# A row-mean kernel: two neighbouring rows per partition, three buffers, and a last block in shrinking chunks

## The chip, the cores and the metric

The kernel runs on one core of one Trainium2 chip. The metric is device time in microseconds (us), the median of several runs. All runs quoted here were classed as fast ones at a full granted clock. A time that is called "in the span" counts from the first instruction of the profiled run; the span is some 1.7 us shorter than the measured time.

Loads and stores go through 16 DMA engines. One load instruction becomes a number of packets on each engine: in the bulk loads of these runs 8, 16 or 64. For each load, and for the final store, the trace also records 16 completion counts; the transfer counts as landed when the last of them has come. DVE is the vector engine, ACT the scalar engine, PE the matrix engine, and SP issues the DMAs.

## The reference

```python
# x: float32, 64 x 256 x 8192 (537 MB, standard normal)
def reference(x):
    return np.mean(x, axis=2)          # 64 x 256
```

There are 16384 rows of 8192 numbers (32 KiB a row). Each number is read once and added up.

## The kernel before

A bulk load brings 128 partitions x 2 rows, 8 MiB. The two rows of a partition lie 128 rows apart in memory. DVE sums the first one, ACT the second one. There are two buffers. The last two row tiles (a tile is one row on each of 128 partitions) are handled apart, and the very last one comes in four chunks through two small buffers.

```python
x_v = x.rearrange("b c s -> (b c) s").rearrange("(t p) s -> p t s", p=P)
# ... cut ...
in_pool   = ctx.enter_context(tc.tile_pool(name="in", bufs=2))
part_pool = ctx.enter_context(tc.tile_pool(name="part", bufs=2))
# ... cut ...
while t < nbulk:                                   # nbulk = T - 2 = 126
    n = min(R, nbulk - t)                          # R = 2
    xt = in_pool.tile([P, n, S], x.dtype)
    nc.sync.dma_start(out=xt[:], in_=x_v[:, t : t + n, :])          # L82
    for j in range(n):
        tt = t + j
        if (tt % 2) == 0:
            dve_reduce(res_d[:, tt : tt + 1], xt[:, j, :])          # tensor_reduce, L61
        else:
            act_reduce(res_a[:, tt : tt + 1], xt[:, j, :])          # activation with accum_out, L70
    t += n
# ... cut ...
xt = in_pool.tile([P, S], x.dtype)
nc.sync.dma_start(out=xt[:], in_=x_v[:, t1, :])                     # L94; halves to DVE and ACT
# ... cut ...
for c in range(4):
    xc = part_pool.tile([P, q], x.dtype)                            # q = 2048
    nc.sync.dma_start(out=xc[:], in_=x_v[:, t2, c * q : (c + 1) * q])   # L108
    fn, dst = targets[c]                                            # DVE, ACT, DVE, ACT
    fn(dst, xc[:])
# add the partial sums of the last tile on DVE and on ACT, transpose res_d and res_a
# on PE into one PSUM tile (adding them), scale on DVE, store 128 rows of 512 bytes (L134)
```

## Time and profile before

| | before |
|---|---|
| median time | 1259.3 us (1259.16 to 1259.45) |
| span of the profiled run | 1257.8 us |
| load queue busy, share of 16 engines | 99.3% |
| DVE busy, ACT busy | 44%, 36% |
| one bulk load lands every | 19.43 us |
| last chunk in use from, to the end of the span | 1252.03 us, 5.78 us |

First the page of the profiled run: the DMA share in 40 slices (9 is 90% or more), the bytes moved in the same slices, the count of packets, and the load queue with packets, MB and share of 16 engines' span.

```profile
DMA  9999999999999999999999999999999999999996
GB/s 402 431 433 434 433 434 434 432 431 426 430 430 434 432 434 433 434 432 431 427 430 430 434 433 432 433 434 432 431 427 431 430 434 431 434 434 433 432 431 259
DMA packets 18004, 536.97 MB, mean 427 GB/s; under 512 B 1104, under 2 KB 1232, under 8 KB 1232
...
q1 hardware_dynamic: 18000, 536.94, 99.3%
```

The loads are the limit from the second slice to the last but one. Only the first and the last slice show a hole.

Next the timeline of DVE in the middle of the run: start, duration, instruction, and in brackets how long it was idle and what ended that.

```profile
605.91 8.69 DVE L61 TENSOR_REDUCE res_d<-xt 128x1 f32<-128x8192 f32 x1 [10.74 <-DMA xt<-in_x_dram]
625.33 8.69 DVE L61 TENSOR_REDUCE res_d<-xt 128x1 f32<-128x8192 f32 x1 [10.74 <-DMA xt<-in_x_dram]
```

DVE waits for each load, and the loads come 19.42 us apart, 8 MiB each: 432 GB/s. In the packet records all bulk packets have 32768 bytes and last 1218 ns (median). DVE frees a buffer 8.7 us after it landed. At that moment the other load has 10.7 us to go, so the refill is queued in time.

The end looks otherwise. This is the chain of waits from 1238 us on (start, duration, what), followed by the busy times of 1240 to 1245 us (the last two columns are the DMA share and GB/s).

```profile
1244.58 0.33 SPq L108
...
1245.01 6.94 DMA xc<-in_x_dram
...
1252.03 2.01 ACT junk L70 x2
...
1254.07 0.30 ACT res_a L115
...
1254.41 0.49 PE resT_ps L128
...
1254.92 0.29 DVE resT L133
```

```profile
1240.00:1245.00 5.00, 0.00 (x0) 0.00 (x0) 4.56 (x2) 3.72 (x4) 0.00 (x0) 1.00 0.21 88
```

The third and fourth chunks of the last tile are issued at 1244.58 and 1245.01 us only, after DVE and ACT have freed the two small buffers. By then the queue has run dry: 88 GB/s in these 5 us. After the last chunk come ACT, ACT, PE, DVE in a row, then the store. The list of DMA issues gives the store's size and its time from issue to landing, 1.5 us:

```profile
out_dram<-resT SPq DMA_DIRECT2D x1, 64.0 KB, 1.5
```

By the timeline of SP it is issued at 1255.24 us:

```profile
1255.24 0.35 SPq L134 DMA_DIRECT2D out_dram<-resT  x1
```

### The profile page before, as it was taken

Reading aid. Unit: us, or ns where it says so; the run is one execution under the profiler, and the core shown is the slowest. Engines: PE = TensorE matmul, PEld = TensorE weight load, DVE = VectorE, ACT = ScalarE, POOL = GpSimd, SP = SyncE. Lnnn points to the kernel's source line nnn. Section 1 sums busy time; section 2 is a strip of 40 time slices with the busy share of each in tenths; the row PEclk is TensorE's granted clock in tenths of the full one; section 3 lists DMA queues with packets and bytes.
Section 4 is the critical chain, followed back from the end, with each engine's and each line's share of the span. In section 5 each row is a group of like instructions: output and inputs, shape, how many; then the busy total and the mean of one; then the engine's idle time right before and its main releaser. Section 6 shows DMA issues by size and latency. Waiting matters only on the chain.

```text
span 1257.8 us, 460 instructions
## 1 busy us (share of the span) xinstructions
PE 0.9 (0%) x2; PEld 0.4 (0%) x2; DVE 556.6 (44%) x68; ACT 458.0 (36%) x134; POOL 1.0 (0%) x8
## 2 busy tenths in 40 slices
PE   0000000000000000000000000000000000000000
PEld 0000000000000000000000000000000000000000
DVE  2354353453543534435345354353443544535435
ACT  2244243342432423424334243243342433424424
POOL 0000000000000000000000000000000000000000
DMA  9999999999999999999999999999999999999996
GB/s 402 431 433 434 433 434 434 432 431 426 430 430 434 432 434 433 434 432 431 427 430 430 434 433 432 433 434 432 431 427 431 430 434 431 434 434 433 432 431 259
DMA packets 18004, 536.97 MB, mean 427 GB/s; under 512 B 1104, under 2 KB 1232, under 8 KB 1232
## 3 DMA queue, kind: packets, MB, share of 16 engines
q1 hardware_dynamic: 18000, 536.94, 99.3%
q14 instruction: 4, 0.03, 0.0%
HBM read 536.87 MB, written 0.07 MB: 427 GB/s over the span
## 4 chain that ended last, share of the span: by engine, by line
DMA 77%; DVE 22%; issue 0%; ACT 0%; SPq 0%; PE 0%; ACTq 0%
DMA xt<-in_x_dram 77%; DVE res_d L61 22%; DMA xc<-in_x_dram 1%; ACT junk L70 0%; SPq L82 0%; PE resT_ps L128 0%; SPq L108 0%; ACT res_a L115 0%; DVE resT L133 0%; SPq L94 0%; ACTq L70 0%
## 5 line engine op out<-in xcount | busy, mean ns | idle before, releaser
L61 DVE TENSOR_REDUCE res_d<-xt 128x1 f32<-128x8192 f32 x64 | 551.6, 8619 | 690.7 <-DMA xt<-in_x_dram 690.7
L70 ACT ACTIVATE junk<-xt 128x8192 f32<-128x8192 f32 x64 | 446.5, 6976 | 765.3 <-DMA xt<-in_x_dram 765.3
L70 ACT ACTIVATION_READ_ACCUMULATOR junk<-xt 128x1 f32 x64 | 11.9, 186 | 0.0
L70 ACT ACT_TABLE_LOAD x1 | 1.3, 1283 | 22.7 <-DMA xt<-in_x_dram 22.7
L70 ACT ACTIVATE junk<-xc 128x2048 f32<-128x2048 f32 x2 | 3.8, 1910 | 8.3 <-DMA xc<-in_x_dram 8.3
L61 DVE TENSOR_REDUCE aux_d<-xc 128x1 f32<-128x2048 f32 x1 | 2.3, 2286 | 4.9 <-DMA xc<-in_x_dram 4.9
L61 DVE TENSOR_REDUCE res_d<-xc 128x1 f32<-128x2048 f32 x1 | 2.3, 2276 | 0.0
L133 DVE TENSOR_SCALAR resT<-resT_ps 128x128 f32<-128x128 f32 x1 | 0.3, 292 | 3.0 <-PE resT_ps L128 3.0
L124 PE MATMUL resT_ps<-ident,res_d 128*128 128x128 f32 x1 | 0.4, 447 | 1252.1 <-DVE res_d L112 1252.1
L124 PEld LDWEIGHTS resT_ps<-ident,res_d 128*128 128x128 f32 x1 | 0.2, 182 | 1252.1 <-issue 1252.1
L128 PE MATMUL resT_ps<-ident,res_a 128*128 128x128 f32 x1 | 0.5, 472 | 1.8 <-ACT res_a L115 1.8
L70 ACT ACTIVATION_READ_ACCUMULATOR junk<-xc 128x1 f32 x2 | 0.4, 187 | 0.0
L115 ACT ACTIVATE res_a<-res_a,aux_a 128x1 f32<-128x1 f32 x1 | 0.3, 295 | 0.0
L48 POOL TENSOR_SCALAR_AFFINE_SELECT ident<-ident 128x128 f32<-128x128 f32 x1 | 0.3, 292 | 0.1
L40 POOL MEMSET res_d<- 128x128 f32 x1 | 0.2, 204 | 0.3 <-POOLq L149 0.3
L41 POOL MEMSET res_a<- 128x128 f32 x1 | 0.2, 204 | 0.0
L47 POOL MEMSET ident<- 128x128 f32 x1 | 0.2, 204 | 0.0
L128 PEld LDWEIGHTS resT_ps<-ident,res_a 128*128 128x128 f32 x1 | 0.2, 183 | 2.1 <-ACT res_a L115 2.1
L112 DVE TENSOR_TENSOR res_d<-res_d,aux_d 128x1 f32<-128x1 f32 x1 | 0.2, 159 | 0.0
L149 POOL MEMSET const-bfloat16-1.0<- 128x1 bf16 x1 | 0.1, 101 | 0.0
L149 POOL MEMSET const-uint8-127<- 128x1 uint8 x1 | 0.1, 101 | 0.0
L149 POOL MEMSET const-float32-0.0<- 128x1 f32 x1 | 0.1, 98 | 0.2 <-issue 0.2
(1 smaller groups left out, 0.1 us busy)
## 6 DMA issues: line engine op xcount, KB each, us to landing
xt<-in_x_dram SPq DMA_DIRECT2D x63, 8192.0 KB, 30.1
xt<-in_x_dram SPq DMA_DIRECT2D x1, 4096.0 KB, 20.9
xc<-in_x_dram SPq DMA_DIRECT2D x4, 1024.0 KB, 15.0
out_dram<-resT SPq DMA_DIRECT2D x1, 64.0 KB, 1.5
```

The source lines that it names most:

```text
L40: nc.gpsimd.memset(res_d[:], 0.0)
L41: nc.gpsimd.memset(res_a[:], 0.0)
L47: nc.gpsimd.memset(ident[:], 0.0)
L48: nc.gpsimd.affine_select(out=ident[:], in_=ident[:], compare_op=mybir.AluOpType.not_equal, fill=1.0, base=0, pattern=[[-1, P]], channel_m ...
L61: nc.vector.tensor_reduce(out=dst, in_=src, axis=mybir.AxisListType.X, op=mybir.AluOpType.add,)
L70: nc.scalar.activation(out=junk[:], in_=src, func=mybir.ActivationFunctionType.Copy, accum_out=dst,)
L112: nc.vector.tensor_add(out=res_d[:, t2 : t2 + 1], in0=res_d[:, t2 : t2 + 1], in1=aux_d[:, 0:1])
L115: nc.scalar.activation(out=res_a[:, t2 : t2 + 1], in_=res_a[:, t2 : t2 + 1], func=mybir.ActivationFunctionType.Identity, bias=aux_a[:, 0:1 ...
L124: nc.tensor.matmul(out=resT_ps[:], lhsT=res_d[:], rhs=ident[:], is_transpose=True, start=True, stop=False,)
L128: nc.tensor.matmul(out=resT_ps[:], lhsT=res_a[:], rhs=ident[:], is_transpose=True, start=False, stop=True,)
L133: nc.vector.tensor_scalar_mul(out=resT[:], in0=resT_ps[:], scalar1=inv)
L149: nc = _bacc.Bacc("TRN2", target_bir_lowering=False, num_devices=1)
```

## The change

The intent: longer contiguous pieces for the loads (64 KiB per partition in place of 2 x 32 KiB), one more buffer so that loads are queued further ahead (ACT writes over its source, which frees the scratch tile's space), and a last block whose loads are all queued at once and shrink toward the end, so that little is left to do after the last byte.

```diff
-    x_v = x.rearrange("b c s -> (b c) s").rearrange("(t p) s -> p t s", p=P)
+    x_v = x.rearrange("b c s -> (b c) s").rearrange("(n p r) s -> n p r s", p=P, r=R)
-    in_pool = ctx.enter_context(tc.tile_pool(name="in", bufs=2))
+    in_pool = ctx.enter_context(tc.tile_pool(name="in", bufs=BULK_BUFS))     # 3
 # ... cut ...
+    def act_sum(dst, src):
+        nc.scalar.activation(out=src, in_=src, func=COPY, accum_out=dst)
+    for n in range(LB):                                                      # LB = 63
+        xt = in_pool.tile([P, R, S], x.dtype, name="xt")
+        nc.sync.dma_start(out=xt[:], in_=x_v[n])
+        dve_sum(res[0][:, n : n + 1], xt[:, 0, :])
+        act_sum(res[1][:, n : n + 1], xt[:, 1, :])
 # ... cut: the last block, one bulk buffer xl: its first row in one load, halves to DVE and ACT
+    for c, w in enumerate(LAST_CHUNKS[:-1]):                # (4096, 2048, 1024, 512, 512)
+        ld = nc.sync.dma_start(out=xl[:, 1, pos : pos + w], in_=x_v[LB, :, 1, pos : pos + w])
+        mid = pos + w // 2                                  # half to DVE, half to ACT
+        dve_sum(fin_in[:, lastw + k : lastw + k + 1], xl[:, 1, pos:mid])
+        act_sum(fin_in[:, lastw + k + 1 : lastw + k + 2], xl[:, 1, mid : pos + w])
 # ... cut: the loop's counters k and pos
+    with tc.issue_after(ld.ins):
+        nc.sync.dma_start(out=fin_in[:, 0:lastw], in_=x_v[LB, :, 1, pos:S])
 # ... cut: the 63 bulk blocks' sums are transposed on PE, scaled on DVE and stored (out_bulk)
+    nc.vector.tensor_scalar(out=fin_in[:, 0 : lastw + k], in0=fin_in[:, 0 : lastw + k],
+        scalar1=inv, scalar2=None, op0=mybir.AluOpType.mult, op1=ADD, accum_out=fin[:, 1:2])
+    nc.sync.dma_start(out=out_last, in_=fin[:])             # 128 pieces of 8 bytes, side by side
```

More of the change, by code (lines that the diff above doesn't have):

```diff
@@ L6 @@
 from concourse._compat import with_exitstack
-TILES_PER_DMA = 2
+ROWS = 2
+BULK_BUFS = 3
+LAST_CHUNKS = (4096, 2048, 1024, 512, 512)
 @with_exitstack
@@ L19 @@
     P = nc.NUM_PARTITIONS
+    F32 = mybir.dt.float32
+    X = mybir.AxisListType.X
+    ADD = mybir.AluOpType.add
+    COPY = mybir.ActivationFunctionType.Copy
     B, C, S = x.shape
     N = B * C
-    assert N % P == 0, (N, P)
-    T = N // P
-    x_v = x.rearrange("b c s -> (b c) s").rearrange("(t p) s -> p t s", p=P)
-    outT_v = out.rearrange("b c -> (b c)").rearrange("(t p) -> t p", p=P)
-    R = TILES_PER_DMA
-    assert T >= 2
-    in_pool = ctx.enter_context(tc.tile_pool(name="in", bufs=2))
-    part_pool = ctx.enter_context(tc.tile_pool(name="part", bufs=2))
-    res_pool = ctx.enter_context(tc.tile_pool(name="res", bufs=1))
-    junk_pool = ctx.enter_context(tc.tile_pool(name="junk", bufs=1))
-    psum_pool = ctx.enter_context(tc.tile_pool(name="psum", bufs=1, space=bass.MemoryType.PSUM))
-    res_d = res_pool.tile([P, T], mybir.dt.float32)
-    res_a = res_pool.tile([P, T], mybir.dt.float32)
-    nc.gpsimd.memset(res_d[:], 0.0)
-    nc.gpsimd.memset(res_a[:], 0.0)
-    aux_d = res_pool.tile([P, 4], mybir.dt.float32)
-    aux_a = res_pool.tile([P, 4], mybir.dt.float32)
-    ident = res_pool.tile([P, P], mybir.dt.float32)
+    R = ROWS
+    assert R == 2 and N % (P * R) == 0, (N, P, R)
+    NB = N // (P * R)
+    LB = NB - 1
+    assert 1 <= LB <= P and sum(LAST_CHUNKS) == S
+    inv = 1.0 / float(S)
+    x_v = x.rearrange("b c s -> (b c) s").rearrange("(n p r) s -> n p r s", p=P, r=R)
+    o_v = out.rearrange("b c -> (b c)")
+    out_bulk = o_v[0 : LB * P * R].rearrange("(n p r) -> n p r", p=P, r=R)
+    out_last = o_v[LB * P * R : N].rearrange("(p r) -> p r", r=R)
+    in_pool = ctx.enter_context(tc.tile_pool(name="in", bufs=BULK_BUFS))
+    res_pool = ctx.enter_context(tc.tile_pool(name="res", bufs=1))
+    psum_pool = ctx.enter_context(
+        tc.tile_pool(name="psum", bufs=1, space=bass.MemoryType.PSUM)
+    )
+    res = [res_pool.tile([P, NB], F32, name=f"res{r}") for r in range(R)]
+    ident = res_pool.tile([P, P], F32)
     nc.gpsimd.memset(ident[:], 0.0)
@@ L56 @@
     )
-    inv = 1.0 / float(S)
-    def dve_reduce(dst, src):
-        nc.vector.tensor_reduce(
-            out=dst,
-            in_=src,
-            axis=mybir.AxisListType.X,
-            op=mybir.AluOpType.add,
-        )
-    def act_reduce(dst, src):
-        junk = junk_pool.tile([P, src.shape[-1]], mybir.dt.float32)
-        nc.scalar.activation(
-            out=junk[:],
-            in_=src,
-            func=mybir.ActivationFunctionType.Copy,
-            accum_out=dst,
-        )
@@ L77 @@
-    nbulk = T - 2
-    t = 0
-    while t < nbulk:
-        n = min(R, nbulk - t)
-        xt = in_pool.tile([P, n, S], x.dtype)
-        nc.sync.dma_start(out=xt[:], in_=x_v[:, t : t + n, :])
-        for j in range(n):
-            tt = t + j
-            if (tt % 2) == 0:
-                dve_reduce(res_d[:, tt : tt + 1], xt[:, j, :])
-            else:
-                act_reduce(res_a[:, tt : tt + 1], xt[:, j, :])
-        t += n
-    t1 = T - 2
-    half = S // 2
-    xt = in_pool.tile([P, S], x.dtype)
@@ L94 @@
-    nc.sync.dma_start(out=xt[:], in_=x_v[:, t1, :])
-    dve_reduce(res_d[:, t1 : t1 + 1], xt[:, 0:half])
-    act_reduce(res_a[:, t1 : t1 + 1], xt[:, half:S])
-    t2 = T - 1
-    q = S // 4
-    targets = [
-        (dve_reduce, res_d[:, t2 : t2 + 1]),
-        (act_reduce, res_a[:, t2 : t2 + 1]),
-        (dve_reduce, aux_d[:, 0:1]),
-        (act_reduce, aux_a[:, 0:1]),
-    ]
-    for c in range(4):
-        xc = part_pool.tile([P, q], x.dtype)
-        nc.sync.dma_start(out=xc[:], in_=x_v[:, t2, c * q : (c + 1) * q])
-        fn, dst = targets[c]
-        fn(dst, xc[:])
@@ L112 @@
-    nc.vector.tensor_add(
-        out=res_d[:, t2 : t2 + 1], in0=res_d[:, t2 : t2 + 1], in1=aux_d[:, 0:1]
-    )
-    nc.scalar.activation(
-        out=res_a[:, t2 : t2 + 1],
-        in_=res_a[:, t2 : t2 + 1],
-        func=mybir.ActivationFunctionType.Identity,
-        bias=aux_a[:, 0:1],
-        scale=1.0,
-    )
-    resT_ps = psum_pool.tile([T, P], mybir.dt.float32)
-    nc.tensor.matmul(
-        out=resT_ps[:], lhsT=res_d[:], rhs=ident[:], is_transpose=True,
-        start=True, stop=False,
-    )
@@ L128, with dve_sum @@
-    nc.tensor.matmul(
-        out=resT_ps[:], lhsT=res_a[:], rhs=ident[:], is_transpose=True,
-        start=False, stop=True,
-    )
-    resT = res_pool.tile([T, P], mybir.dt.float32)
-    nc.vector.tensor_scalar_mul(out=resT[:], in0=resT_ps[:], scalar1=inv)
-    nc.sync.dma_start(out=outT_v, in_=resT[:])
+    def dve_sum(dst, src):
+        nc.vector.tensor_reduce(out=dst, in_=src, axis=X, op=ADD)
+    def act_sum(dst, src):
+        nc.scalar.activation(out=src, in_=src, func=COPY, accum_out=dst)
@@ new lines @@
+    for n in range(LB):
[3 more added lines that the diff above has]
+        act_sum(res[1][:, n : n + 1], xt[:, 1, :])
+    nparts = 2 * len(LAST_CHUNKS)
+    lastw = LAST_CHUNKS[-1]
+    xl = in_pool.tile([P, R, S], x.dtype, name="xt")
+    fin_in = res_pool.tile([P, lastw + nparts], F32)
+    fin = res_pool.tile([P, R], F32)
+    head = res_pool.tile([P, 2], F32)
+    half = S // 2
@@ new lines @@
+    nc.sync.dma_start(out=xl[:, 0, :], in_=x_v[LB, :, 0, :])
+    dve_sum(head[:, 0:1], xl[:, 0, 0:half])
+    act_sum(head[:, 1:2], xl[:, 0, half:S])
+    pos, k = 0, 0
+    for c, w in enumerate(LAST_CHUNKS[:-1]):
+        ld = nc.sync.dma_start(
+            out=xl[:, 1, pos : pos + w], in_=x_v[LB, :, 1, pos : pos + w]
+        )
+        mid = pos + w // 2
+        dve_sum(fin_in[:, lastw + k : lastw + k + 1], xl[:, 1, pos:mid])
+        act_sum(fin_in[:, lastw + k + 1 : lastw + k + 2], xl[:, 1, mid : pos + w])
+        k += 2
+        pos += w
@@ new lines @@
+    with tc.issue_after(ld.ins):
+        nc.sync.dma_start(out=fin_in[:, 0:lastw], in_=x_v[LB, :, 1, pos:S])
+    nc.vector.tensor_scalar(
+        out=head[:],
+        in0=head[:],
+        scalar1=inv,
+        scalar2=None,
+        op0=mybir.AluOpType.mult,
+        op1=ADD,
+        accum_out=fin[:, 0:1],
+    )
+    bulk = res_pool.tile([P, P, R], F32)
+    for r in range(R):
+        ps = psum_pool.tile([P, P], F32, name=f"ps{r}")
+        nc.tensor.transpose(out=ps[:LB, :], in_=res[r][:, 0:LB], identity=ident[:])
+        nc.vector.tensor_scalar_mul(out=bulk[:LB, :, r], in0=ps[:LB, :], scalar1=inv)
@@ L138 @@
+    nc.sync.dma_start(out=out_bulk, in_=bulk[:LB])
+    nc.vector.tensor_scalar(
+        out=fin_in[:, 0 : lastw + k],
+        in0=fin_in[:, 0 : lastw + k],
+        scalar1=inv,
+        scalar2=None,
+        op0=mybir.AluOpType.mult,
+        op1=ADD,
+        accum_out=fin[:, 1:2],
+    )
+    nc.sync.dma_start(out=out_last, in_=fin[:])
 _INS = ['x']
```

## The prediction

> **What bounds the kernel now.** The DMA engines. The page's queue table has the load queue busy for 99.3% of 16 engines' span, 427 GB/s on average; DVE is busy for 44%, ACT for 36%. The 40 slices show 426 to 434 GB/s, but 402 in the first and 259 in the last. In the chain of waits an 8 MiB load lands every 19.43 us (431.8 GB/s). A buffer is refilled 8.7 us (the DVE reduction) after it lands, while 10.7 us of the other load are still queued, so the queue never runs dry in the bulk. In the packet records every bulk packet is 32768 bytes and takes 1218 ns (median).
>
> **What the change does.**
>
> 1. *Descriptors.* Two neighbouring rows make one contiguous 64 KiB run per partition: 8 packets per engine and load in place of 16. Packets of 8192 bytes take 309 ns (median), of 32768 1218: a line through both gives 6 ns per packet. Eight packets saved, times 63 loads, times 6 ns: 3.0 us. [...] Estimate: 3.2 us, all on the critical path.
>
> 2. *Third buffer, sums in place.* They remove nothing critical: 0. ACT's 7.03 us stays off the path.
>
> 3. *End of the loading.* Before, the last row's chunks share two buffers: the third load waits for a DVE reduction, the fourth is issued at 1245.01 us after ACT, and the windows show 88 GB/s in 1240 to 1245 us. With a full queue the last chunk would land 9.75 us (4 MiB) after 1237.9, at 1247.7, not 1252.03. The change queues all the last block's loads ahead: -4.3 us; smaller chunks cost +0.2.
>
> 4. *After the last byte.* Before, 1252.03 to 1257.8 us: ACT 2.01 (two instructions), ACT 0.30, PE 0.49, DVE 0.29, then some 2.6 of output issue, landing and exit. After: one DVE instruction over 520 elements, estimated 0.7 us from 2.29 for 2048, then the same 2.6. Transposes and bulk output finish while the last block loads. -2.4 us, less 0.1 for 8-byte output pieces.
>
> 5. *Start.* Unchanged: the first load is in at 22.7 us.
>
> **Sum.** 1259.3 - 3.2 - 4.3 + 0.2 - 2.3 = 1249.7 us, 0.8% less. Range for 8 in 10: 1246.5 to 1252.5. Faster by over 2%: 1%; within 2%: 97%; slower by over 2%: 2%.
>
> **What the profile would show.** Load packets of 65536 bytes, about 2430 ns each; a load landing every 19.38 us; no low slice before the end, and no DMA issue of the last block waiting for DVE or ACT of the same block; the last load landing about 1244.8 us into the span; 3.4 us from there to the end.
>
> **What would make it wrong.** The run is cut back into 32 KiB packets, or longer packets cost proportionally as much (about 1253). Reading partitions 64 KiB apart is slower or faster in HBM: 1% of rate is 12 us. One engine lags and the last small chunk waits for it. The bulk output delays the final one. ACT's small sums, each with a 0.19 us accumulator read, end later than DVE's.

## The result, and the profile after

The changed kernel takes 1249.59 us (median of 4 runs, 1249.44 to 1249.93), against 1259.30 us before (4 runs). A ratio here is the mean time of one kernel's fast runs over the mean of the other's of the same rounds, so it is not quite the ratio of the two medians. It is 0.9923, with a 95% interval of 0.9909 to 0.9937. The predicted 1249.7 us is met within 0.1 us. The question is whether it was met for the right reasons.

The same lines of the page, for the changed kernel:

```profile
DMA  9999999999999999999999999999999999999997
GB/s 403 437 437 437 437 437 437 422 420 435 437 437 437 437 437 435 437 426 418 435 437 437 437 437 437 433 437 428 418 435 437 437 437 437 435 433 437 431 418 336
DMA packets 10156, 536.97 MB, mean 430 GB/s; under 512 B 1257, under 2 KB 1320, under 8 KB 1704
...
q1 hardware_dynamic: 10152, 536.94, 99.5%
```

There are some 7800 fewer packets. Don't read the single slices too finely: they jump between 418 and 437 GB/s while the loads go on landing evenly. The timeline of DVE is the better measure:

```profile
603.77 8.69 DVE L61 TENSOR_REDUCE res<-xt 128x1 f32<-128x8192 f32 x1 [10.66 <-DMA xt<-in_x_dram]
623.13 8.69 DVE L61 TENSOR_REDUCE res<-xt 128x1 f32<-128x8192 f32 x1 [10.67 <-DMA xt<-in_x_dram]
```

A load now lands every 19.35 us (19.36 between these two). The packets have 65536 bytes and last 2422 ns (median).

The end, from the timeline of SP and from the chain of waits, then the same 5 us of busy times:

```profile
1193.42 0.33 SPq L80 DMA_DIRECT2D xt<-in_x_dram  x1
1193.80 1.85 SPq L86 DMA_DIRECT2D xt<-in_x_dram  x4
1195.69 0.43 SPq L95 DMA_DIRECT2D fin_in<-in_x_dram  x1
```

```profile
1195.69 47.63 DMA fin_in<-in_x_dram
...
1243.46 0.69 DVE fin_in L114
```

```profile
1240.00:1245.00 5.00, 0.00 (x0) 0.00 (x0) 3.71 (x6) 2.74 (x8) 0.00 (x0) 1.00 0.41 152
```

All six loads of the last block are issued by 1196 us, some 47 us before the last of them lands at 1243.32. The 152 GB/s are no hole in the loading any more: the loading itself ends within these 5 us. One DVE instruction follows, at 1243.46. Then the store, first from the timeline, then from the list of DMA issues:

```profile
1244.19 0.37 SPq L123 DMA_DIRECT2D out_dram<-fin  x1
```

```profile
out_dram<-fin SPq DMA_DIRECT2D x1, 1.0 KB, 3.1
```

This store is 64 times smaller than the one before, and takes 3.1 us to land where the other took 1.5.

The three stretches of the two spans, cut at the same events (the start of the first reduction, of the last full block's, and of the instruction that uses the last chunk):

| stretch | before, us | after, us | change | predicted |
|---|---|---|---|---|
| to the first reduction | 22.71 | 22.68 | 0.0 | 0 |
| 62 more bulk loads | 1205.0 | 1200.7 | -4.3 | -3.2 |
| last block, to the use of its last chunk | 24.3 | 20.1 | -4.2 | -4.1 |
| from there to the end | 5.8 | 4.7 | -1.1 | -2.3 |
| sum | 1257.8 | 1248.2 | -9.7 | -9.6 |

Two terms of the sum were off by more than 1 us each, in opposite directions. (These are single executions, and the profiled one of the changed kernel was the slowest of its four, 1249.93 us against 1249.44 for the fastest, so a few tenths of a us in a stretch mean little.) The experiments ask what sets each term.

### The profile page after: what moved, and what is told of

Its sections match the earlier page's. It is cut to its first block, busy times and chain, and to the rows that moved or that the text cites. A ratio compares the mean times of both kernels' runs of the same rounds, so it can differ in the third digit from the quotient of the medians.

```text
span 1248.2 us, 464 instructions
## 1 busy us (share of the span) xinstructions
PE 0.9 (0%) x2; PEld 0.4 (0%) x2; DVE 557.5 (45%) x74; ACT 458.0 (37%) x137; POOL 0.7 (0%) x6
## 4 chain that ended last, share of the span: by engine, by line
DMA 85%; DVE 15%; SPq 0%; issue 0%; DVEq 0%
DMA xt<-in_x_dram 81%; DVE res L61 15%; DMA fin_in<-in_x_dram 4%; SPq L86 0%; DVE fin_in L114 0%; SPq L68 0%; SPq L80 0%; DVEq L114 0%; DVEq L149 0%
## 5 line engine op out<-in xcount | busy, mean ns | idle before, releaser
L61 DVE TENSOR_REDUCE res<-xt 128x1 f32<-128x8192 f32 x63 | 547.2, 8686 | 684.8 <-DMA xt<-in_x_dram 684.8
L64 ACT ACTIVATE xt<-xt 128x8192 f32<-128x8192 f32 (+2 forms) x68 | 450.5, 6625 | 784.4 <-DMA xt<-in_x_dram 784.3
L64 ACT ACTIVATION_READ_ACCUMULATOR xt<-xt 128x1 f32 x68 | 12.7, 187 | 0.0
L61 DVE TENSOR_REDUCE fin_in<-xt 128x1 f32<-128x2048 f32 (+3 forms) x4 | 4.6, 1154 | 0.8 <-DMA xt<-in_x_dram 0.6
L61 DVE TENSOR_REDUCE head<-xt 128x1 f32<-128x4096 f32 x1 | 4.4, 4420 | 0.2 <-DMA xt<-in_x_dram 0.2
```

Source lines behind the costliest of these rows:

```text
L61: nc.vector.tensor_reduce(out=dst, in_=src, axis=X, op=ADD)
L64: nc.scalar.activation(out=src, in_=src, func=COPY, accum_out=dst)
```

## The experiments

Every kernel was timed beside the kernel before on the same chip (medians of 1259.15 to 1259.39 us there). The starting theory: a fixed cost per packet explains the bulk, queueing ahead explains the last block, and the third buffer does nothing.

### Rows apart again (e1_rows_apart)

```diff
-    ... .rearrange("(n p r) s -> n p r s", p=P, r=R)
+    ... .rearrange("(n r p) s -> n p r s", p=P, r=R)
```

> The changed kernel, but the two rows that a partition takes in a bulk load lie 128 rows apart in memory, as before the change: packets of 32768 bytes again, everything else (three buffers, sums in place, the new end) kept. The output is in the wrong order on purpose. Theory A (a fixed cost of about 9 ns per packet): a load lands every 19.43 us instead of 19.35, 1249.6 + 62 x 0.07 = 1254.0 us. Rival B (the gain of the bulk came from the third buffer, not from the packets): stays at 1249.6.

Measured: 1254.33 us (1254.10 to 1254.94). All bulk packets have 32768 bytes again. The timeline of DVE:

```profile
605.61 8.69 DVE L61 TENSOR_REDUCE res<-xt 128x1 f32<-128x8192 f32 x1 [10.74 <-DMA xt<-in_x_dram]
625.03 8.69 DVE L61 TENSOR_REDUCE res<-xt 128x1 f32<-128x8192 f32 x1 [10.74 <-DMA xt<-in_x_dram]
```

The loads are 19.42 us apart again, with three buffers. The bulk gain came from the rows, not from the buffer. But "two rows that are neighbours" means two things at once: longer packets, and longer contiguous reading in memory.

### Neighbouring rows, but a cut in the destination (e2_cut_dest)

```diff
-        xt = in_pool.tile([P, R, S], x.dtype, name="xt")
-        nc.sync.dma_start(out=xt[:], in_=x_v[n])
+        xt = in_pool.tile([P, R, S + 16], x.dtype, name="xt")
+        nc.sync.dma_start(out=xt[:, :, 0:S], in_=x_v[n])
 # ... cut: the sums and the last block leave out the gap in the same way
```

> The changed kernel with the same neighbouring rows read, 64 KiB in a piece from memory, but each partition's buffer has a gap of 64 bytes between the two rows, so that no packet can be longer than 32768 bytes. Theory A (cost per packet): 1254.0 us, a load every 19.43 us, as in the run with rows apart. Rival C (longer contiguous reading in memory is what is faster, whatever the packets): 1249.6 us, 19.35 us per load.

Measured: 1253.77 us (1253.70 to 1254.27), correct output. The packets have 32768 bytes though 64 KiB in a piece are read. Of every three loads in the middle of the run, two land 19.43 or 19.44 us after the one before and one 19.37; the median of all 62 periods is 19.42:

```profile
605.96 8.69 DVE L61 TENSOR_REDUCE res<-xt 128x1 f32<-128x8192 f32 x1 [10.74 <-DMA xt<-in_x_dram]
625.40 8.69 DVE L61 TENSOR_REDUCE res<-xt 128x1 f32<-128x8192 f32 x1 [10.75 <-DMA xt<-in_x_dram]
644.77 8.69 DVE L61 TENSOR_REDUCE res<-xt 128x1 f32<-128x8192 f32 x1 [10.69 <-DMA xt<-in_x_dram]
```

It is the packets that count, not the neighbourhood in memory. The reading order is that of the changed kernel, and the gain is gone. (The gap also moves the second row within the buffer. The run before this one, and the one with packets of 8 KiB below, have no gap and show the cost too.)

### Two buffers (e3_two_bufs)

```diff
-BULK_BUFS = 3
+BULK_BUFS = 2
```

> The changed kernel with two bulk buffers in place of three. Theory: the queue holds 10.7 us of work at each refill, so nothing changes, 1249.6 us, within 0.4, and the end of the loading too. Rival B (the third buffer carries part of the gain): above 1251 us, with gaps in the DMA or a later landing of the last block.

Measured: 1249.77 us (1249.57 to 1250.19), correct. The last block's loads are now issued later, between 1212.85 and 1215.55 us, but that is still 28 us before the last chunk lands. The timeline of SP:

```profile
1212.85 0.33 SPq L80 DMA_DIRECT2D xt<-in_x_dram  x1
1213.23 1.85 SPq L86 DMA_DIRECT2D xt<-in_x_dram  x4
1215.12 0.43 SPq L95 DMA_DIRECT2D fin_in<-in_x_dram  x1
```

The third buffer carries none of the gain.

### The rows alone, in the kernel before (e4_before_pairs)

```diff
+    x_pair = x.rearrange("b c s -> (b c) s").rearrange("(n p r) s -> n p r s", p=P, r=2)
-        nc.sync.dma_start(out=xt[:], in_=x_v[:, t : t + n, :])
+        nc.sync.dma_start(out=xt[:], in_=x_pair[t // 2])
```

> The kernel before with one part of the change alone: each bulk load takes two neighbouring rows per partition (64 KiB packets); two buffers, scratch tile and the old end stay. Output in the wrong order on purpose. Theory A: 62 x 0.07 = 4.3 us off, 1255.0 us. Rival B (third buffer): 1259.3, unchanged.

Measured: 1254.81 us (1254.40 to 1255.18), 4.5 us less than the kernel before. The period of the changed kernel is there, with two buffers and with the scratch tile:

```profile
603.66 8.69 DVE L62 TENSOR_REDUCE res_d<-xt 128x1 f32<-128x8192 f32 x1 [10.66 <-DMA xt<-in_x_dram]
623.00 8.69 DVE L62 TENSOR_REDUCE res_d<-xt 128x1 f32<-128x8192 f32 x1 [10.66 <-DMA xt<-in_x_dram]
```

The first part of the change gives its 4.3 us alone as well as together with the rest.

### Packets of 8 KiB (e7_8k)

The cost per packet is small, so it is multiplied here.

```diff
+    x_h = x.rearrange("b c (h s) -> (b c h) s", h=4).rearrange("(n q p) s -> n p q s", p=P, q=8)
-        nc.sync.dma_start(out=xt[:], in_=x_v[n])
+        nc.sync.dma_start(out=xt[:].rearrange("p r (h s) -> p (r h) s", h=4), in_=x_h[n])
```

> The changed kernel with each bulk load cut into eight separate pieces of 8192 bytes per partition, read from distant places (quarters of rows; wrong output on purpose): 64 packets per engine and load in place of 8. The two periods so far, 19.43 us with 16 packets and 19.35 with 8, lie on 19.28 us plus 9 ns per packet. Theory A: a load every 19.28 + 64 x 0.009 = 19.86 us, so 1249.6 + 62 x 0.51 = 1281 us. If the line through the packet durations of the prediction holds (6 ns per packet): 1249.6 + 62 x 56 x 0.006 = 1270.4 us. If the packets' number is not what counts: 1254.

Measured: 1282.94 us (1282.89 to 1283.03), 1.9% slower than the kernel before.

```profile
599.95 8.69 DVE L64 TENSOR_REDUCE res<-xt 128x1 f32<-128x8192 f32 x1 [11.21 <-DMA xt<-in_x_dram]
619.83 8.69 DVE L64 TENSOR_REDUCE res<-xt 128x1 f32<-128x8192 f32 x1 [11.20 <-DMA xt<-in_x_dram]
```

A load lands every 19.88 us. Theory A said 19.86, and the 6 ns of the prediction's line would have given 19.35 + 56 x 0.006 = 19.69. The medians of all 62 periods of a run are 19.351 us with 8 packets per engine (the changed kernel), 19.425 with 16 (the kernel before) and 19.879 with 64. From 8 to 16 that is 9.3 ns per packet, from 8 to 64 it is 9.4 ns. The places that are read changed here too, but the first two runs, with rows apart and with neighbouring rows, show the same median period at 32 KiB (19.43 and 19.42 us). Carried on to no packets at all, this line gives 19.351 - 8 x 0.0094 = 19.276 us for 8 MiB, which is 435.2 GB/s. This is an estimate from the three medians; no run measured it. By it, the changed kernel's bulk (19.351 us) is within 0.4% of a load that costs nothing per packet.

### Four chunk buffers, in the kernel before (e5_before_chunk_bufs)

```diff
-    part_pool = ctx.enter_context(tc.tile_pool(name="part", bufs=2))
+    part_pool = ctx.enter_context(tc.tile_pool(name="part", bufs=4))
```

> The kernel before with four chunk buffers in place of two, nothing else. Theory (the dry queue of the last row costs 4.3 us): all four chunk loads are issued together with the last full row, the last chunk lands at about 1247.7 us into the span, 1259.3 - 4.3 = 1255.0 us. Rival (the small loads are slow in themselves, or the 4.3 us come from something else in the changed end): more than 1257 us.

Measured: 1255.29 us (1255.14 to 1255.35), correct, 3.9 us less than the kernel before. The busy times of the same 5 us as above, then the timeline's line of ACT on the last chunk:

```profile
1240.00:1245.00 5.00, 0.00 (x0) 0.00 (x0) 4.43 (x2) 3.58 (x4) 0.00 (x0) 1.00 1.01 419
```

```profile
1247.77 1.91 ACT L70 ACTIVATE junk<-xc 128x2048 f32<-128x2048 f32 x1 [2.92 <-DMA xc<-in_x_dram]
```

The hole of 88 GB/s is now 419 GB/s, and ACT starts on the last chunk at 1247.77 us in place of 1252.03. One digit in the kernel before would have given 40% of the whole change's gain. By the trace's completion counts the four 1 MiB loads land 2.4 to 2.5 us apart, some 423 GB/s. In this trace a load queued behind another pays no fixed cost that would show: at the 432 GB/s of the bulk 1 MiB takes 2.43 us.

### The final store: without the store ahead of it (e8_no_bulk_out)

The last term of the sum missed by 1.2 us, and the store takes 1.5 us more to land. Three runs change only the stores. First the store of the bulk results is taken out:

```diff
-    nc.sync.dma_start(out=out_bulk, in_=bulk[:LB])
```

> The changed kernel without the store of the 63 blocks' results (wrong output on purpose): the final store of 128 pieces of 8 bytes goes out alone. In the changed kernel it landed 3.06 us after its issue, against 1.55 us for the store of 128 pieces of 512 bytes in the kernel before. Theory D (pieces of 8 bytes are slow to land): still 3.06 us, total 1249.6 us. Rival E (the store of the other results, just ahead on the same engines, holds it up): 1.6 us to landing, total 1248.1 us.

Measured: 1249.77 us (1249.34 to 1250.47).

```profile
out_dram<-fin SPq DMA_DIRECT2D x1, 1.0 KB, 2.9
```

The other store is not what holds it up. Rival E falls.

### The final store: pieces of 512 bytes (e9_out_512)

```diff
-    nc.sync.dma_start(out=out_bulk, in_=bulk[:LB])
-    nc.sync.dma_start(out=out_last, in_=fin[:])
+    nc.sync.dma_start(out=o_v.rearrange("(p s) -> p s", p=P), in_=fin_in[:, 0:P])
```

> As the run without the bulk store, but the final store writes the whole output in 128 pieces of 512 bytes, as the kernel before did, at the same point of the program and from a tile that the same last instruction writes (wrong values on purpose). Theory D: lands 1.55 us after issue, total 1249.6 - 1.5 = 1248.1 us. Rival E: the same time as the run without the bulk store. If a store here takes 3 us whatever its pieces, both are wrong: 1249.6 us.

Measured: 1248.55 us (1248.10 to 1248.85), no overlap with the run above from the same batch.

```profile
out_dram<-fin_in SPq DMA_DIRECT2D x1, 64.0 KB, 1.5
```

At the same place in the program, 64 times the bytes land in half the time.

### The final store: pieces of 8 bytes, far apart (e10_out_8_spread)

```diff
-    nc.sync.dma_start(out=out_bulk, in_=bulk[:LB])
-    nc.sync.dma_start(out=out_last, in_=fin[:])
+    nc.sync.dma_start(out=o_v.rearrange("(p s) -> p s", p=P)[:, 0:2], in_=fin[:])
```

> As the run without the bulk store, with the same 128 pieces of 8 bytes, but laid 512 bytes apart in the output, not side by side (wrong output on purpose). Theory D1 (a piece of 8 bytes is slow whatever its place): lands about 3.06 us after issue, 1249.6 us. Theory D2 (neighbouring pieces in the same stretch of memory wait for each other): nearer to 1.6 us after issue, 1248.1 us.

Measured: 1248.28 us (1248.04 to 1248.63).

```profile
out_dram<-fin SPq DMA_DIRECT2D x1, 1.0 KB, 1.4
```

The same 128 pieces of 8 bytes land in 1.4 us when they are 512 bytes apart. So theory D as first stated ("pieces of 8 bytes are slow to land") is wrong. In these runs the small pieces are slow only when many of them go side by side into one stretch of memory, 128 of them into 1 KB: 2.9 us to landing in the run without the bulk store, 3.1 in the changed kernel and in the run with packets of 8 KiB, against 1.4 here, far apart. The landing is near the 1.6 us that D2 expected. In the changed kernel the packets themselves are out by 1245.3 us, and the 16 completion counts come in one by one from 1245.46 to 1247.26. In the kernel before, all 16 came within 0.2 us. That the pieces wait for each other, as D2 has it, is the author's explanation and was not shown: no run shows whether or where they wait, or how close together they must lie for it.

### The last block stored through a transpose (e11_last_transposed)

```diff
-    nc.sync.dma_start(out=out_last, in_=fin[:])
+    nc.tensor.transpose(out=fin_ps[:], in_=fin[:], identity=ident[:])
+    nc.vector.tensor_copy(out=fin_row[:], in_=fin_ps[:])
+    nc.sync.dma_start(out=out_last, in_=fin_row[:])       # 2 pieces of 512 bytes
 # ... cut: the two new tiles, and x_last in place of x_v for the last block's loads
```

The last block's rows are taken 128 apart for it, which costs nothing that would show, since these rows are loaded one by one anyway: the last chunk lands at 1243.05 us, against 1243.32 in the changed kernel.

> A version meant to beat both: the changed kernel, with the last block's two sums per partition transposed by PE and stored as two pieces of 512 bytes in place of 128 neighbouring pieces of 8 bytes (the last block's rows are taken 128 apart for that; correct output). Adds a PE matmul of about 0.5 us and a DVE copy of about 0.35, saves about 1.5 us of landing: 1249.6 - 0.6 = 1249.0 us. If small stores of few pieces are slow as well: 1250.4 us.

Measured: 1248.99 us (1248.44 to 1249.11), correct, ratio to the kernel before 0.9917 (0.9903 to 0.9930). The timeline at the end:

```profile
1243.20 0.69 DVE L117 TENSOR_SCALAR_CACHE_REDUCE fin_in<-fin_in 128x520 f32<-128x520 f32 x1 [0.35 <-DMA fin_in<-in_x_dram]
...
1243.95 0.37 PE L128 MATMUL fin_ps<-ident,fin 128*2 128x128 f32 x1 [11.58 <-DVE fin_in L117]
1244.37 0.28 DVE L129 COPY fin_row<-fin_ps 2x128 f32<-2x128 f32 x1 [0.47 <-PE fin_ps L128]
1244.67 0.26 SPq L130 DMA_DIRECT2D out_dram<-fin_row  x1
```

PE and DVE add about 0.7 us ahead of the issue. The store then lands at 1245.78 us by the trace's completion counts, 1.1 us after its issue. The version beats both kernels, the changed one by 0.6 us, though that one was timed in another batch. The total is the expected one, but its terms are not: 0.7 us more and 2.0 us less of landing would make 1.2 us. The profiled execution is this version's fastest (1248.44 us) and that of the changed kernel its slowest, so the terms are rough.

### DVE alone on most of the bulk (e12_dve_bulk)

```diff
-        dve_sum(res[0][:, n : n + 1], xt[:, 0, :])
-        act_sum(res[1][:, n : n + 1], xt[:, 1, :])
+        if n < LB - 2:
+            dve_sum(res_all[:, :, n], xt[:])      # both rows in one instruction
+        else:
+            dve_sum(res[0][:, n : n + 1], xt[:, 0, :])
+            act_sum(res[1][:, n : n + 1], xt[:, 1, :])
```

This run is the transposed version with the edit above (res_all holds the sums of both rows in one tile).

> As the transposed version, but DVE alone sums both rows of all bulk blocks but the last two, in one instruction per block, so that ACT has some 120 instructions less. It tests a second thing: in the changed kernel four instruction fetches of 8192 bytes each hold up one DMA engine by about 0.4 us, and at the end 13 engines are done 0.5 to 1.1 us ahead of three. Theory F (these fetches make the laggards, and fewer instructions mean fewer fetches): one or more fetches gone, the last landing 0.3 to 0.8 us earlier, 1248.4 us. Also shows whether the third buffer carries a DVE of 17.4 us per block within a load's 19.35 us: if not, far above 1250 us. If the laggards have another cause: 1249.0 us, as the run beside it.

Measured: 1248.44 us (1248.08 to 1248.69), correct, ratio 0.9914 (0.9900 to 0.9927).

```profile
603.20 17.22 DVE L65 TENSOR_REDUCE res_all<-xt 128x2 f32<-128x16384 f32 x1 [2.13 <-DMA xt<-in_x_dram]
622.55 17.22 DVE L65 TENSOR_REDUCE res_all<-xt 128x2 f32<-128x16384 f32 x1 [2.13 <-DMA xt<-in_x_dram]
```

DVE alone keeps up, 17.22 us in every 19.35, with three buffers. In the packet records the fetches of instructions during the run went from four to two (at 742.6 and 878.4 us). But the last chunk's last completion count came at 1243.00 us, against 1243.05 in the transposed version, so the last laggard is still there. Theory F is confirmed in one half (fewer instructions, fewer fetches) and missed in the other: the landing did not move by the expected 0.3 to 0.8 us. The traces show a little more. In the transposed version three counts of the last chunk are late (1242.48, 1242.82 and 1243.05, the others by 1242.19); here only two are (1242.39 and 1243.00, the others by 1242.07). And the load that lands after the fetch at 414 us is late, against the median period, by 0.38 us in the changed kernel and by 0.23 in the transposed version; here that fetch is gone and the delay with it. So in these traces the fetches do hold up loads, but the last count, which sets the landing, was not that of the laggard that went. The medians of the two versions differ by 0.5 us and their ranges overlap. Whether this version is the faster one stays open.

## Why the prediction was right or wrong

The time was right: 1249.59 us against 1249.7. The list of causes was right too, but two sizes were wrong, by 1.1 and 1.2 us, and made up for each other. That the sum was met within 0.1 us is luck.

1. **Bound by the DMA engines: right.** The load queue was busy for 99.3% of the span, and what changed the time changed the loading or the very end of the chain.
2. **Descriptors, -3.2 us: right mechanism, too small.** The run with the cut destination shows that packets are the cause. The term that was mis-sized is "6 ns per packet", from a line through the durations of 8 KiB and 32 KiB packets. It measured 9.3 to 9.4 ns per packet in the median period of the loads. That would be 4.6 us over 62 loads; the stretch shows -4.3, since a few loads in each run land some tenths of a us late. In these traces a packet's recorded duration is not the time that it takes from the engine: 16 x 1218 ns is 19.49 us, more than the period of 19.43, so the records of successive 32 KiB packets overlap. Of the 3.2 us on record, 3.0 come from that line; the other 0.2 were the author's estimate, and no trace shows them.
3. **Third buffer and sums in place, 0: right.** With two buffers the changed kernel takes the same time within 0.2 us. The sums in place were not undone alone, but the kernel before reaches the same period with its scratch tile.
4. **End of the loading, -4.3 + 0.2 us: right.** -4.2 in the spans. More chunk buffers alone give 3.9 in the kernel before. The 0.2 for smaller chunks was the author's estimate and was not tested by itself.
5. **After the last byte, -2.3 us: half of it.** Up to the issue of the store, the step went as predicted: 3.21 us before, 0.73 after. The term that was mis-sized is "less 0.1 for 8-byte output pieces", the author's estimate. It measured 1.5 us, as the landing of the store went from 1.55 to 3.07 us after issue. The runs show that neither the store ahead of it (2.9 us without it) nor the 8 bytes as such (1.4 us far apart) are the reason, but that the pieces are neighbours in one stretch of 1 KB.
6. **What the profile would show.** Packets of 65536 bytes: yes, 2422 ns each (predicted 2430). A load every 19.38 us: 19.35. The last load at about 1244.8 us: 1243.32. From there to the end 3.4 us: 4.8.

Of the listed dangers, one happened in small, unasked for in the sum: some engines lag. 13 of the 16 completion counts of the last chunk come between 1241.96 and 1242.29 us, the other three at 1242.76, 1243.04 and 1243.32. After the first 100 us, just three bulk packets last 2700 ns or more (2796 to 3080, in place of 2422), each 0.3 us after an instruction fetch of 8192 bytes has started. The load that lands next is 0.11 to 0.38 us late, against the median period. The fourth fetch falls into the last block, and 0.3 us after its start an 8 KiB packet lasts 681 ns, in place of 312. That these fetches make the laggards is shown in part: the last run removed two of four fetches, and one of three laggards went, in one profiled execution. The last laggard stayed, so what the fetches cost in the end is open.

## What to carry to other kernels

When a kernel is bound by loads, measure the cost of a packet from how far apart whole loads land, at two packet sizes, and not from the durations of single packets: here the loads gave 9.3 to 9.4 ns per packet and the durations 6, and the records of successive 32 KiB packets overlap (16 x 1218 ns are 19.49 us, in a period of 19.43). Look at the end of the run by itself: a short queue of small buffers can let the loading run dry there (88 GB/s for 5 us here), and the cure may be one digit (3.9 us less here). The small store at the very end was on the critical path in full here (3.1 us), and how its pieces lie beside each other mattered more than how many bytes it has: 1 KB landed in 2.9 to 3.1 us side by side and in 1.4 far apart, 64 KB in 1.5.
